# Residual sum kept in PSUM, and the norm placed right behind its root, at the entry of two feed-forward layers

## The chip, the cores and the metric

One core of a Trainium2 chip runs the whole program in a single launch. The metric is device time in microseconds (us), from which a median of three runs is taken. Five engines work side by side, each with its own in-order queue: TensorE (PE in the profile, with its weight loads as PEld), VectorE (DVE), ScalarE (ACT), GpSimd (POOL) and SyncE (SP), which here only starts transfers. Matmuls write to PSUM, the accumulator memory; the other data live in SBUF.

## The reference

Two transformer layers on one sequence of 1024 tokens with 1024 features, all in float32. The change sits where each layer goes from its token mixer to its feed-forward part:

```python
x = x + diff_attention(h, ...)        # layer 0;  layer 1: x + mla_attention(h, ...)
h = rms_norm(x, ffn_norm_g[i])
x = x + conv_ffn(h, w_up, conv_w, conv_b, w_down)

def rms_norm(x, g):
    xf = x.astype(float32)
    y = xf * rsqrt(mean(xf * xf, axis=-1, keepdims=True) + 1e-6)
    return y * g
```

The last step of each mixer is a product of its output with a 1024 by 1024 matrix `w_o`. So for each tile of 128 tokens the kernel needs the residual sum (x plus that product), its mean of squares, the normed tile, and the tile's transpose, which is the moving operand of the up-projection. The residual sum itself is needed again after the feed-forward part, and goes to HBM until then.

## The kernel before, in words

Every float32 product is made from three matmuls of a split operand: a high part (`self.hi`, a cast, line 127, on ACT as a rule) and a low part (`self.lo`, the difference, line 130, on DVE or POOL). Lines 119 to 121 (`mm3`) are the three matmuls. The up-projection is a Strassen-like scheme of seven products, so that operands which are sums and differences of blocks must be built too: `T1` to `T4` on the side of the tokens, `S1` to `S4` on the side of the weights.

The change is in `project_rest`, which runs once in each layer (about 510 to 570 us and 1680 to 1740 us of the span). Before it, half of the output product has been added to `X`. `project_rest` makes the other half, for the eight token tiles in the order 0, 4, 1, 5, 2, 6, 3, 7 (`tiles`). Iteration n of its loop handles three tiles at once:

- for tile n-2 (`older`), whose norm exists: PE transposes it (`turn`, line 812, eight 128x128 transposes into two PSUM banks), and the banks are split into operands. A tile of the first half of the tokens (`a_tile`) gives `B11` and `B21`: two casts on ACT (`high`) and two differences on DVE (`low`). A tile of the second half gives `B12` and `B22`: ACT copies B12 out (line 830), DVE forms `T1`, `T3`, `T2` and, for the first two of these tiles, `T4` (`sub`, line 843), and T1 is split at once, the low part on POOL; layer 1 does so with T2 as well.
- for tile n-1 (`before`): DVE adds the product in PSUM to the residual and writes the sum to SBUF (`add`, line 847), SP stores the sum to `x_d` (line 850), ACT sums its squares (`squares`, line 157), DVE takes the mean plus epsilon (line 164) and POOL the power -1/2 (`root`, line 167), and DVE multiplies sum, root and gain (line 916): the norm.
- for tile n: PE makes 24 matmuls into a two-bank PSUM tile (`ys[n] = self.big()`; there are two such tiles), behind the transposes of tile n-2.

Inside the loop the order on PE, DVE and POOL is the order of the program; the order on ACT and SP is planned by the scheduler from the dependencies. An instruction that waits holds up all that is behind it on its engine. On DVE the order in iteration n is: add, the first differences (low B11, or T1 and T3), line 164, the rest (low B21, or low B22, T2 and T4), one weight sum S in iterations 3 to 6 (line 1013), and then the norm. The sum lives in one of two SBUF places (`totals`); the norm goes to another place (`home`). The places of `totals` are used after the loop for split weights: the cast `w2h` of the closing order (a list of tokens, `CLOSE`, which begins behind the loop) writes where tile 6's sum was, and so it waits for that sum's store.

Tile 7 has no place in the loop any more: its sum, squares, root and norm are tokens of `CLOSE`, in halves.

Of the kernel before, what the change touches and what calls it, by code (L numbers as in the profile page):

```python
# [13 lines left out]
ALU = mybir.AluOpType  # L14
# [42 lines left out]
class Trunk:  # L57
# [28 lines left out]
    def at(self, place, shape, dt=F32):  # L86

        if isinstance(place, str):
            return self.t(self.mem, place, shape, 1, dt)
        size = int(np.prod(shape[1:]))  # L90
        piece = place[: shape[0], :size]
        if dt != F32:
            piece = piece.bitcast(dt)
        if len(shape) == 3:
            piece = piece.rearrange("p (a b) -> p a b", b=shape[2])
        return piece
# [684 lines left out]
    def project_rest(self, W, o_d, os, X, at, home, x_d, g, junk, places, sums, early, begin):  # L781
# [5 lines left out]
        nc = self.nc  # L787
        dve, gp = nc.vector, nc.gpsimd
# [3 lines left out]
        T, raws, ys, banks, tmp, r, ends = {}, {}, {}, {}, {}, {}, {}  # L792
# [3 lines left out]
        def load(n):  # L796
            if n < NT:
                raws[n] = self.project_load(tiles[n], ks, o_d, raw)

        def parts(n):  # L800
            return self.project_parts(raws.pop(n), ks, W, os)

        def normed(i, cols):
            return ends[cols.start] if i == NT - 1 else X[i][:, cols]

        def turn(i, which=3):
            names = ("B11", "B21") if i < 4 else ("B12", "B22")
            for name, cols in list(zip(names, (first, rest)))[which == 2 : which]:
                ps = banks[name, i % 4] = self.bank("u" if name == "B22" else "b")
                x = normed(i, cols)  # L810
                for k in range(4):
                    nc.tensor.transpose(ps[:, k * P : (k + 1) * P], x[:, k * P : (k + 1) * P], self.ident)

        def source(name, q):
            return cut(banks[name, q] if name[0] == "B" else tmp[name, q])

        def dst(name, q, part):
            if name not in T:
                T[name] = [self.at(place, [P, 4, 512], F32R) for place in places[name]]
            return T[name][part][:, :, q * P : (q + 1) * P]  # L820

        def high(name, q):
            self.hi(dst(name, q, 0), source(name, q))

        def low(name, q, eng=dve):
            self.lo(dst(name, q, 1), source(name, q), dst(name, q, 0), eng)

        def copy(q):
            tmp["B12", q] = sums([P, 512])
            nc.scalar.copy(tmp["B12", q], banks["B12", q])  # L830

        def sub(name, q):
            x, y = {
                "T1": lambda: (tmp["B12", q], banks["B11", q]),
                "T3": lambda: (banks["B22", q], tmp["B12", q]),
                "T2": lambda: (banks["B22", q], tmp["T1", q]),
                "T4": lambda: (banks["B21", q], tmp["T2", q]),
            }[name]()
            if name == "T1":
                tmp[name, q] = sums([P, 512])  # L840
            else:
                tmp[name, q] = normed(*{"T2": (q, first), "T3": (q + 4, first), "T4": (q + 4, rest)}[name])
            dve.tensor_sub(tmp[name, q], x, y)

        def add(i, y, cols=slice(0, D)):
            x, to = X[i]
            dve.tensor_add(to[:, cols], x[:, cols], y[:, cols])

        def store(i):
            nc.sync.dma_start(x_d[i * P : (i + 1) * P, :], X[i][1])  # L850

        def both(name, q, eng=dve):
            high(name, q)
            low(name, q, eng)
# [8 lines left out]
        for n, i in enumerate(tiles):  # L863
            into, ys[n] = ready, self.big()
            before = tiles[n - 1] if n else None
            older = tiles[n - 2] if n > 1 else None
            if older is not None:
                q, a_tile = older % 4, older < 4
                turn(older)
            into(ys[n][:, first], 0)  # L870
            into(ys[n][:, rest], 512)
            load(n + 2)
            if n + 1 < NT:
                ready = parts(n + 1)
            if before is None:
                continue
            X[before] = X[before], at(before, X[before])
            add(before, ys[n - 1])
            store(before)
            if older is not None:  # L880
                if a_tile:
                    high("B11", q)
                else:
                    copy(q)
                    if q or "B22" in early:
                        high("B22", q)
            s = self.squares(X[before][1], junk)
            if older is not None:
                if a_tile:
                    high("B21", q)  # L890
                    if older == 1 and "B22" not in early:
                        both("B22", 0)
                    low("B11", q)
                else:
                    sub("T1", q)
                    sub("T3", q)
            r[before] = self.root(s, D)
            if n in (4, 5):
                start.part(n - 4)
            if older is not None:  # L900
                if a_tile:
                    low("B21", q)
                else:
                    both("T1", q, gp)
                    if q or "B22" in early:
                        low("B22", q)
                    sub("T2", q)
                    if q < 2:
                        sub("T4", q)
                    if "T2" in early:  # L910
                        both("T2", q, gp)
            for name in {3: ("S1",), 4: ("S2",), 5: ("S4",), 6: ("S3",)}.get(n, ()):
                start.sum_of(0, name)
            x, total = X[before]
            X[before] = home(before, x)
            dve.scalar_tensor_tensor(X[before], total, r.pop(before), g, ALU.mult, ALU.mult)

        last, st = ys[NT - 1], SimpleNamespace()

# [1398 lines left out]
```

## Time and profile before

| | |
|---|---|
| median of 3 runs | 2379.11 us (2378.89 to 2379.76) |
| the profiled execution | 2379.93 us, of which the span from first to last instruction is 2378.1 us |
| granted TensorE clock | 0.999 of full speed |
| busy: PE, PEld, DVE, ACT, POOL | 2346.4, 1975.7, 1925.3, 1246.5, 587.5 us |
| line 916 (the norm), 14 times | min 1271, median 1572, max 2318 ns |

In a timeline row the columns are: start in us, duration in us, engine, line, operation, output<-inputs, count and, in brackets, how long the engine was idle before it and what released it. Names there are those of the places or banks: `u`, `s` and `h` are SBUF places, `S` is the two-bank PSUM tile, `b` is a PSUM bank. `u` is also the tag of one more PSUM bank (the one that takes B22), so that a `u` can be either. DVE instructions overlap a little: the next starts some 0.08 us before the end of the one before.

### The profile page before, as it was taken

The page shows a single profiled execution, that of the slowest core. Times are in us where ns is not written, and L with a number is a line of the kernel's source. Part 1 is how long each engine was busy: PE and PEld are TensorE (multiplying, and loading weights), DVE is VectorE, ACT ScalarE, POOL GpSimd, SP SyncE. Part 2 cuts the span into 40 slices and gives each one's busy share as a digit, 9 for nine tenths or more (in the row PEclk, how much of TensorE's full clock was granted, in tenths as well). Part 3 has the DMA queues.
Part 4 walks back from the last instruction along what each step waited for, and adds up shares of the span by engine and source line. Part 5 has one row for each costly group of instructions (what it writes and reads, how often), then busy time and mean ns, then how long its engine had stood idle before and what let it go on. Part 6 is the DMA issues. An engine that isn't in the chain of part 4 may idle for free.

```text
span 2378.1 us, 32958 instructions
## 1 busy us (share of the span) xinstructions
PE 2346.4 (99%) x12146; PEld 1975.7 (83%) x12146; DVE 1925.3 (81%) x3170; ACT 1246.5 (52%) x2301; POOL 587.5 (25%) x465
## 2 busy tenths in 40 slices
PE   9999999999999999999999999999999999999998
PEld 7888888788888888888898889988788888888886
DVE  6777877859888888999855888886588888889997
ACT  5666666745444444354444778775354444443544
POOL 4545444324000000000133666673420000000001
PEclk9999999999999999999999999999999999999999
DMA  3111111342222222652221211133322222227502
GB/s 148 40 36 36 49 37 54 114 130 86 93 84 80 80 88 81 233 176 84 84 98 56 72 33 39 41 98 114 108 72 94 82 80 80 89 80 283 177 1 80
DMA packets 95667, 213.42 MB, mean 90 GB/s; under 512 B 8713, under 2 KB 33937, under 8 KB 95505
## 3 DMA queue, kind: packets, MB, share of 16 engines
q1 hardware_dynamic: 86304, 183.51, 23.6%
q10 hardware_dynamic: 9200, 27.80, 3.2%
q8 instruction: 96, 1.57, 0.3%
q14 instruction: 67, 0.54, 0.1%
HBM read 158.85 MB, written 52.43 MB: 89 GB/s over the span
## 4 chain that ended last, share of the span: by engine, by line
PE 89%; DVE 5%; DMA 2%; ACT 2%; issue 1%; POOL 0%; POOLq 0%; DVEq 0%; ACTq 0%; SPq 0%
PE S L119 13%; PE S L121 13%; PE S L120 13%; PE b L119 9%; PE b L120 8%; PE b L121 8%; PE u L119 5%; PE u L121 4%; PE u L120 4%; PE S L1866 3%; PE b L263 2%; PE u L2022 1%; PE u L2021 1%; PE b L1912 1%; DVE s L130 1%
## 5 line engine op out<-in xcount | busy, mean ns | idle before, releaser
L167 POOL TENSOR_TENSOR st<-st,mhalf 128x1 f32<-128x1 f32 x56 | 35.4, 633 | 1301.5 <-DVE st L164 1291.4
L121 PE MATMUL S<-s,u 128*128 128x512 f32 (+1 forms) x800 | 301.3, 377 | 1.1 <-POOL u L130 1.0
L119 PE MATMUL S<-s,u 128*128 128x512 f32 (+1 forms) x800 | 301.8, 377 | 0.2 <-ACT u L1092 0.2
L120 PE MATMUL S<-s,u 128*128 128x512 f32 (+1 forms) x800 | 301.0, 376 | 0.0
L127 ACT CAST u<-h 128x512 fp32r<-128x512 f32 (+1 forms) x194 | 115.8, 619 | 274.4 <-DVE h L1013 262.2
L119 PE MATMUL b<-s,u 128*128 128x512 f32 x588 | 230.8, 393 | 1.1 <-DVE u L130 0.4
L120 PE MATMUL b<-s,u 128*128 128x512 f32 x588 | 229.0, 389 | 0.0
L121 PE MATMUL b<-s,u 128*128 128x512 f32 x588 | 229.0, 389 | 0.0
L1070 DVE SCALAR_TENSOR_TENSOR u<-u,conv,u 128x1023 f32<-128x1023 f32 (+1 forms) x176 | 225.0, 1278 | 0.8 <-ACT u L1066 0.7
L149 POOL TENSOR_TENSOR u<-u,st 128x512 f32<-128x512 f32 (+7 forms) x160 | 173.2, 1091 | 161.4 <-DVE st L2007 107.5
L127 ACT CAST s<-u 128x512 fp32r<-128x512 f32 (+3 forms) x229 | 144.0, 663 | 97.8 <-PE u L121 28.3
L127 ACT CAST u<-b 128x512 fp32r<-128x512 f32 (+1 forms) x256 | 134.8, 547 | 92.1 <-PE b L1912 57.7
L130 DVE TENSOR_TENSOR u<-b,u 128x512 fp32r<-128x512 f32 (+1 forms) x256 | 158.5, 631 | 23.7 <-ACT u L127 22.6
L121 PEld LDWEIGHTS S<-s,u 128*128 128x128 f32 x800 | 150.5, 188 | 29.2 <-POOL u L130 1.4
L119 PEld LDWEIGHTS S<-s,u 128*128 128x128 f32 x800 | 150.5, 188 | 27.9 <-ACT u L1092 0.5
L120 PEld LDWEIGHTS S<-s,u 128*128 128x128 f32 x800 | 150.6, 188 | 27.2
L119 PE MATMUL u<-s,s 128*128 128x512 f32 (+1 forms) x408 | 165.2, 405 | 1.1 <-DVE s L130 0.9
L121 PE MATMUL u<-s,s 128*128 128x512 f32 (+1 forms) x408 | 158.3, 388 | 0.0
L120 PE MATMUL u<-s,s 128*128 128x512 f32 (+1 forms) x408 | 157.6, 386 | 0.0
L130 DVE TENSOR_TENSOR s<-u,s 128x512 fp32r<-128x512 f32 (+2 forms) x205 | 140.7, 720 | 16.4 <-ACT s L127 15.9
L1073 ACT ACTIVATE u<-u 128x1024 f32<-128x1024 f32 x44 | 46.7, 1062 | 187.6 <-DVE u L1070 187.6
L130 DVE TENSOR_TENSOR u<-h,u 128x512 fp32r<-128x512 f32 x171 | 117.9, 689 | 32.4 <-ACT u L127 31.5
(290 smaller groups left out, 6384.9 us busy)
## 6 DMA issues: line engine op xcount, KB each, us to landing
u<-in_ffn_up SPq DMA_DIRECT2D x88, 512.0 KB, 4.2
g_d<-u ACTq DMA_DIRECT2D x44, 512.0 KB, 2.6
u<-in_ffn_down SPq DMA_DIRECT2D x66, 256.0 KB, 4.9
u<-g_d SPq DMA_DIRECT2D x62, 256.0 KB, 3.9
s<-in_da_wqkv SPq DMA_DIRECT2D x23, 512.0 KB, 3.3
x_d<-u SPq DMA_DIRECT2D x16, 512.0 KB, 3.0
s<-x_d SPq DMA_DIRECT2D x8, 1024.0 KB, 10.8
s<-g_d SPq DMA_DIRECT2D x18, 256.0 KB, 5.3
```

What stands on the lines that cost most here:

```text
L119: mm(out, lh, rl, start=first, stop=False, skip_group_check=onto)
L120: mm(out, lh, rh, start=False, stop=False, skip_group_check=onto)
L121: mm(out, ll, rh, start=False, stop=last, skip_group_check=onto)
L127: self.nc.scalar.copy(out, src)
L130: (eng or self.nc.vector).tensor_sub(out, src, hi.bitcast(F32))
L149: self.nc.gpsimd.tensor_mul(x, x, s.to_broadcast(list(x.shape)))
L167: nc.gpsimd.tensor_tensor(r, s, self.mhalf, ALU.pow)
L263: self.nc.tensor.transpose(ps[:, j * P : (j + 1) * P], probs[t][:, k : k + P], self.ident)
L1070: nc.vector.scalar_tensor_tensor(t[half][:, back:], u[half][:, : S - back], w, t[half][:, back:], ALU.mult, ALU.add)
L1073: nc.scalar.activation(t[0], t[0], AF.Silu)
L1866: nc.tensor.matmul(sc[c][:, b : b + m], q[rows, qp, qs], kt[rows, kp, :m], start=x == 0, stop=x == 2)
L1912: k.nc.tensor.transpose(ps[:, j * P : (j + 1) * P], self.e[t][0][:, c : c + P], k.ident)
```

## The change

The sum of tile n-1 is no longer written to SBUF by DVE. DVE adds the residual into the PSUM tile (`total`), ACT takes the squares from there and then copies the sum to its SBUF place, from which it is stored; the norm reads the PSUM tile too. The norm is moved up: for a second-half tile it now stands in front of T2, T4 and S, for a first-half tile in front of S. Tile 7, in the closing order, is as before.

```diff
-            X[before] = X[before], at(before, X[before])
-            add(before, ys[n - 1])
-            store(before)
+            total = ys[n - 1]
+            dve.tensor_add(total, X[before], total)
...
-            s = self.squares(X[before][1], junk)
+            s = self.squares(total, junk)
+            X[before] = X[before], at(before, X[before])
+            nc.scalar.copy(X[before][1], total)
+            store(before)
...
             r[before] = self.root(s, D)
             if n in (4, 5):
                 start.part(n - 4)
+
+            def norm():
+                X[before] = home(before, X[before][0])
+                dve.scalar_tensor_tensor(X[before], total, r.pop(before), g, ALU.mult, ALU.mult)
+
             if older is not None:
                 if a_tile:
                     low("B21", q)
                 else:
                     both("T1", q, gp)
                     if q or "B22" in early:
                         low("B22", q)
+                    norm()
                     sub("T2", q)
                     if q < 2:
                         sub("T4", q)
                     if "T2" in early:
                         both("T2", q, gp)
+            if older is None or older < 4:
+                norm()
             for name in {3: ("S1",), 4: ("S2",), 5: ("S4",), 6: ("S3",)}.get(n, ()):
                 start.sum_of(0, name)
-            x, total = X[before]
-            X[before] = home(before, x)
-            dve.scalar_tensor_tensor(X[before], total, r.pop(before), g, ALU.mult, ALU.mult)
```

## The prediction

> **What bounds the kernel now.** I read the page first, then PE's list of waits, then PE's timeline around the waits found there, and last the timelines of DVE, ACT and POOL beside it. On the page the busy line and the chain that ended last say which engine to follow:
>
> ```profile
> span 2378.1 us, 32958 instructions
> PE 2346.4 (99%) x12146; PEld 1975.7 (83%) x12146; DVE 1925.3 (81%) x3170; ACT 1246.5 (52%) x2301; POOL 587.5 (25%) x465
> PE 89%; DVE 5%; DMA 2%; ACT 2%; issue 1%; POOL 0%; POOLq 0%; DVEq 0%; ACTq 0%; SPq 0%
> ```
>
> PE is idle for about 2378.1 - 2346.4 = 32 us in all. An edit on other engines can win only such idle time. The longest total in the list of PE's waits is the one at issue:
>
> ```profile
> PE b L812 <- DVE u L916: 4.6, 4, 1.3
> ```
>
> The transposes (L812) waited four times for a norm (L916), 4.6 us. Idle time counts from the modelled end of a matmul, so I take what was lost from starts. First layer 0, then layer 1: the last matmul before a set of transposes, and the first transpose.
>
> ```profile
> 527.63 0.40 PE L121 MATMUL S<-s,h 128*128 128x512 f32 x1
> 527.87 0.60 PE L812 MATMUL b<-ident,u 128*128 128x128 f32 x4
> ...
> 534.00 0.39 PE L121 MATMUL S<-s,h 128*128 128x512 f32 x1
> 534.50 1.06 PE L812 MATMUL b<-ident,u 128*128 128x128 f32 x8
> ...
> 547.14 0.39 PE L121 MATMUL S<-s,h 128*128 128x512 f32 x1
> 548.87 1.06 PE L812 MATMUL b<-ident,u 128*128 128x128 f32 x8 [1.34 <-DVE u L916]
> ```
>
> ```profile
> 1702.15 0.39 PE L121 MATMUL S<-s,h 128*128 128x512 f32 x1
> 1703.86 1.06 PE L812 MATMUL b<-ident,u 128*128 128x128 f32 x8 [1.31 <-DVE u L916]
> ...
> 1716.51 0.39 PE L121 MATMUL S<-s,h 128*128 128x512 f32 x1
> 1718.22 1.06 PE L812 MATMUL b<-ident,u 128*128 128x128 f32 x8 [1.33 <-DVE u L916]
> ...
> 1730.71 0.39 PE L121 MATMUL S<-s,h 128*128 128x512 f32 x1
> 1731.69 1.06 PE L812 MATMUL b<-ident,u 128*128 128x128 f32 x8 [0.60 <-DVE u L916]
> ```
>
> Unhindered, the step is 527.87 - 527.63 = 0.24. The others are 0.50, 1.73, 1.71, 1.71 and 0.98, so 0.26 + 1.49 + 1.47 + 1.47 + 0.74 = 5.43 us are lost. All but the last come behind an iteration that ends with a weight sum; the large ones follow second-half tiles. The unhindered period of an iteration on PE is 534.24 - 527.87 = 6.37 us.
>
> Why the norm is late shows on DVE in iteration 5 of layer 0, with the ACT and POOL rows that it waits for or runs beside:
>
> ```profile
> 541.08 1.22 DVE L847 TENSOR_TENSOR u<-s,S 128x1024 f32<-128x1024 f32 x1 [0.17 <-PE S L121]
> 542.27 0.69 DVE L843 TENSOR_TENSOR h<-h,b 128x512 f32<-128x512 f32 x1
> ...
> 543.81 0.15 DVE L164 TENSOR_SCALAR st<-st 128x1 f32<-128x1 f32 x1 [0.25 <-ACT u L157]
> 543.88 0.68 DVE L130 TENSOR_TENSOR s<-u,s 128x512 fp32r<-128x512 f32 x1
> 544.48 0.68 DVE L843 TENSOR_TENSOR u<-u,h 128x512 f32<-128x512 f32 x1
> 545.20 0.69 DVE L843 TENSOR_TENSOR u<-b,u 128x512 f32<-128x512 f32 x1
> 545.80 0.68 DVE L1013 TENSOR_TENSOR h<-u,h 128x512 f32<-128x512 f32 x1
> 546.40 2.32 DVE L916 SCALAR_TENSOR_TENSOR u<-u,st,u 128x1024 f32<-128x1024 f32 x1
> 548.64 1.21 DVE L847 TENSOR_TENSOR u<-s,S 128x1024 f32<-128x1024 f32 x1
> ```
>
> ```profile
> 540.90 0.62 ACT L127 CAST h<-h 128x512 fp32r<-128x512 f32 x1 [3.61 <-issue]
> ...
> 542.62 1.07 ACT L157 ACTIVATE u<-u 128x1024 f32<-128x1024 f32 x1
> 543.58 0.20 ACT L157 ACTIVATION_READ_ACCUMULATOR u<-u 128x1 f32 x1
> ```
>
> ```profile
> 544.04 0.55 POOL L167 TENSOR_TENSOR st<-st,mhalf 128x1 f32<-128x1 f32 x1 [1.16 <-DVE st L164]
> ...
> 545.82 1.82 POOL L130 TENSOR_TENSOR s<-h,s 128x512 fp32r<-128x512 f32 x1
> ```
>
> The root is ready at 544.04 + 0.55 = 544.59, but the norm starts at 546.40, behind T2, T4 and S4, and then takes 2.32 us beside a POOL subtraction. From add to add this iteration costs DVE 548.64 - 541.08 = 7.56 us, more than PE's 6.37.
>
> **The change, part by part.** *The norm reads PSUM.* Whether that shortens it is told by DVE rows beside POOL, and by a row of the same operation with one operand in PSUM:
>
> ```profile
> 531.36 0.69 DVE L843 TENSOR_TENSOR u<-b,u 128x512 f32<-128x512 f32 x1
> 531.96 1.20 DVE L1013 TENSOR_TENSOR h<-u 128x512 f32<-128x512 f32 x1
> ```
>
> ```profile
> 531.32 1.30 POOL L130 TENSOR_TENSOR s<-h,s 128x512 fp32r<-128x512 f32 x1
> ```
>
> ```profile
> L439 DVE SCALAR_TENSOR_TENSOR u<-u,st,S x2: 1275/1278/1280, 7.2 to 8.4; 128x1024 f32<-128x1024 f32 x2
> ```
>
> Both DVE rows start under the POOL row. The one with a PSUM input keeps its 0.69, the one with two SBUF inputs takes 1.20 instead of 0.68. So I take 1.28 us for every norm, with 2.32 as the other end, and 1.20 for an S that lands beside POOL. The Trainium skill, page "SBUF — State Buffer", section "Who interferes with whom", says that a DVE instruction with two SBUF inputs contends with a GpSimd one that reads SBUF, and one with at most one SBUF input doesn't; these rows agree. By that rule the norm would be 1.28, without it 2.32 wherever POOL follows the root.
>
> *The norm is moved up.* It passes T2 and T4 (second-half tiles) and S. What it passes becomes later by the norm's 1.2 us: T4 frees the bank that the next first-half tile's B21 goes to, four transposes into its set, some 0.4 us behind the norm's own need.
>
> *The sum goes to PSUM in place.* Removed: the SBUF write of 14 adds. The add keeps its 1.22 us by row 541.08, which reads PSUM and writes SBUF. No row shows a DVE add that writes PSUM; the nearest is that row, and the other end is two passes, 2.44 us. I take 1.22. Squares from PSUM: at their 1.07 from SBUF; a 128x1024 activation out of `S` stands in this row at 1.118, so between 0 and +0.05 us each:
>
> ```profile
> L1891 ACT ACTIVATE u<-S,st 128x1024 f32<-128x1024 f32 x16 | 17.9, 1118 | 12.6 <-DVE st L1880 12.5
> ```
>
> *Added: 14 ACT copies of 128x1024*, at about 1.1 us by that row. ACT is half idle, so the copy matters only for who waits on it. First the norm: whether it may read the tile beside the copy no row shows; it starts at the end of the root at the earliest, at the end of the copy at the latest, 0.3 us apart (below). I take the later. Second the T1 cast behind it on ACT, whose product comes only behind the loop. Third the PSUM tile: it is free only when norm and copy are done, but the transposes in front of its next matmuls need the norm anyway: nothing. Fourth the store: it leaves some 2.4 us later (squares, copy). Behind it on SP stand loads of the next operands; the cast of one runs at 540.90 and its product only behind the transposes of 548.87, so 2.4 us are covered. The other user of the store is a rival below.
>
> *The walk.* Second-half iteration, from the add's start (rows of iteration 5): T1 and T3 end at 2.4; squares are read at 543.78 - 541.08 = 2.7; root ready at 3.5; copy 2.7 to 3.8; norm 3.9 to 5.2; T2, T4, S at 0.6 each: done at 6.9, against 7.56. First-half iteration, with two rows of iteration 6:
>
> ```profile
> 550.15 0.69 DVE L130 TENSOR_TENSOR s<-b,s 128x512 fp32r<-128x512 f32 x1 [0.30 <-ACT s L127]
> ...
> 551.69 0.15 DVE L164 TENSOR_SCALAR st<-st 128x1 f32<-128x1 f32 x1 [0.84 <-ACT u L157]
> ```
>
> The mean at 551.69 - 548.64 = 3.05, copy until 4.1, norm 4.2 to 5.4, S until 6.0. A pair takes DVE 6.9 + 6.0 = 12.9 us; PE takes 2 x 6.37 = 12.7. So the big stalls go, since norms end at 5.2 to 5.4 and are needed at about 6.2, but DVE runs up to half a microsecond behind PE. Late next are T4 in front of B21 (at 6.4 plus that lag, needed at 6.7) and the norm of iteration 6: I put 0.3 us per layer, 0.3 more in layer 1 where T2 is split on POOL and meets S, and 0.2 for the end of layer 1, where tile 7's chain starts earlier against PE by less than the 0.74 won: 1.1 us, at most 2.
>
> Sum: 5.43, and about 0.03 of slower restart behind each of five stalls (an estimate), 0.15, make 5.6 us on offer; less 1.1 that is 4.5 us. Both layers' following stages are PE's, so all of it reaches the end. The profiled execution took 2379.93, 0.82 above the median 2379.11; it would become 2375.4, the median 2374.6. A measurement of this kernel tells a difference of about 0.2%, 4.8 us, from none: the bound is 2374.35, just beside my value.
>
> **The rivals.** *All is won.* Copy and norm overlap, or the lag never reaches PE: 5.6 us, 2373.5. For it: without the wait for the copy a pair costs 12.9 - 2 x 0.3 = 12.3, under 12.7. Against it the Trainium skill, page "PSUM — Partial Sum Buffer", section "PSUM bank collisions raise a hardware error", has a rule: two engines may not touch one bank at once, two reads included. By it copy and norm must stand one behind the other, as I took for the sum; no run here shows it.
>
> *The later store holds up ACT.* The cast `w2h` waits for the store of tile 6's sum, and ACT's plan has it in front of the last copy of B12:
>
> ```profile
> 554.69 0.62 ACT L127 CAST u<-h 128x512 fp32r<-128x512 f32 x1 [3.04 <-DMA x_d<-u]
> 555.90 0.59 ACT L830 COPY h<-b 128x512 f32<-128x512 f32 x1 [0.59 <-PE b L812]
> ```
>
> ```profile
> DMA to landing us min/median/max: 2.6/3.0/5.9
> ```
>
> Now ACT is free 555.90 - 555.31 = 0.59 us before it is needed. With the store 2.4 us later and PE unhindered, the copy, the squares and the norm of tile 3 would come late by 0.6 to 3.5 us (landing 3.0 to 5.9) in each layer: 2 us twice, 2378.5. The planner orders ACT anew and will more likely put the cast behind the squares.
>
> *The wait is only handed on.* If ACT puts the 0.62 T1 cast in front of the copy, a pair costs 13.5, 0.8 over PE's; three pairs in two layers give 4.8 us back: 2379.
>
> *Slower.* The add in place reads and writes the same bank. With e us more per add a pair costs 12.9 + 2e, and six pairs lose 6 x (0.2 + 2e): the gain of 5.6 is gone at e = 0.37. With two passes (1.22) it is 6 x 2.6 = 15.8 - 5.6 = 10 us slower, 2389. Against it: plain adds into other places show no such cost.
>
> **How the numbers follow.** My case 0.45 (2373.8 to 2375.5), all won 0.20, the store 0.16, handed on 0.10, slower 0.09. Of my own case a bit over half lies below 2374.35, so faster 0.2 + 0.25 = 0.45; same 0.20 + 0.16 + 0.10 = 0.46; slower 0.09. The range of eight in ten runs from 2373.0, under which all stalls of the list are not enough, to 2379.2.
>
> **What would show it.** Right: no L812 waits for L916 over 0.3 us; norms all at 1.28; an ACT copy of 1.1 right behind each squares; adds still 1.22; S rows at 1.2 where POOL runs. Wrong: adds near 2.4; L812 waiting for L843 (T4) or for ACT's copy by over 1 us; an ACT row waiting for `x_d` ahead of the last L830 and a late norm of tile 3.

## The result, and the profile after

The changed kernel takes 2374.59 us, the median of 12 runs (2373.11 to 2376.89). The kernel before, run beside it, takes 2379.80 (2378.06 to 2381.29). The ratio is 0.9979 with a 95% interval of 0.9972 to 0.9987: about 5.2 us faster, just over the 0.2% that a measurement tells from no change. The profiled execution took 2374.86 us (before: 2379.93), at the same granted clock of 0.999. From its page, the span, the busy line and the chain that ended last:

```profile
span 2373.1 us, 32978 instructions
PE 2345.3 (99%) x12146; PEld 1975.3 (83%) x12146; DVE 1919.9 (81%) x3170; ACT 1259.3 (53%) x2315; POOL 584.3 (25%) x465
PE 91%; DVE 5%; DMA 1%; ACT 1%; issue 1%; POOL 0%; POOLq 0%; DVEq 0%; SPq 0%; ACTq 0%
```

The span is 5.0 us shorter and PE's busy time 1.1: most of what went, 3.9 us, is PE's idle time. In the list of PE's waits the entry of 4.6 us for the norm is gone (the norm is now line 905), and the transposes wait only at these places:

```profile
PE u L812 <- DVE h L945: 0.7, 2, 0.4
PE b L812 <- DVE u L843: 0.5, 1, 0.5
```

L945 is tile 7's norm in the closing order. PE's timeline, at the place that lost 1.49 us before, at the iteration behind it, and at the end of layer 1:

```profile
547.05 0.40 PE L121 MATMUL S<-s,h 128*128 128x512 f32 x1
547.28 1.04 PE L812 MATMUL b<-ident,u 128*128 128x128 f32 x8
...
553.42 0.39 PE L121 MATMUL S<-s,h 128*128 128x512 f32 x1
553.65 0.60 PE L812 MATMUL b<-ident,u 128*128 128x128 f32 x4
...
1725.97 1.03 PE L812 MATMUL b<-ident,u 128*128 128x128 f32 x8
...
1730.21 0.63 PE L812 MATMUL u<-ident,h 128*128 128x128 f32 x4 [0.33 <-DVE h L945]
```

The steps are 0.23 now, and 553.65 - 547.28 = 6.37 is the unhindered period. All fourteen such steps in the two loops read 0.23 or 0.24. DVE, ACT and POOL in the same iterations as those shown of before:

```profile
541.15 1.23 DVE L878 TENSOR_TENSOR S<-s,S 128x1024 f32<-128x1024 f32 x1 [0.81 <-PE S L121]
...
544.68 1.28 DVE L905 SCALAR_TENSOR_TENSOR u<-S,st,u 128x1024 f32<-128x1024 f32 x1 [0.22 <-ACT u L888]
...
547.21 0.68 DVE L1020 TENSOR_TENSOR h<-u,h 128x512 f32<-128x512 f32 x1
547.81 1.22 DVE L878 TENSOR_TENSOR S<-s,S 128x1024 f32<-128x1024 f32 x1
...
550.27 0.15 DVE L164 TENSOR_SCALAR st<-st 128x1 f32<-128x1 f32 x1 [0.65 <-ACT u L157]
...
551.25 1.28 DVE L905 SCALAR_TENSOR_TENSOR u<-S,st,u 128x1024 f32<-128x1024 f32 x1 [0.23 <-ACT u L888]
552.46 0.68 DVE L1020 TENSOR_TENSOR h<-u,u 128x512 f32<-128x512 f32 x1
553.85 1.23 DVE L878 TENSOR_TENSOR S<-s,S 128x1024 f32<-128x1024 f32 x1 [0.71 <-PE S L121]
```

```profile
543.55 1.03 ACT L888 COPY u<-S 128x1024 f32<-128x1024 f32 x1
...
554.28 0.59 ACT L830 COPY h<-b 128x512 f32<-128x512 f32 x1 [3.13 <-PE b L812]
554.77 0.63 ACT L127 CAST u<-h 128x512 fp32r<-128x512 f32 x1
```

```profile
544.46 1.29 POOL L130 TENSOR_TENSOR u<-u,u 128x512 fp32r<-128x512 f32 x1
```

The norm starts at 544.68, under a POOL subtraction that began at 544.46, and takes 1.28 us; before, it started 1.8 us later behind its add and took 2.32. DVE now waits for PE in front of the add (0.81, 0.71), where PE waited for DVE before.

The following table is worked out from the starts of transposes (L812) in the profiled executions. "Loop" runs from the first transposes of iteration 2 to those of tile 3 behind the loop, "tail" from there to the first ones of tile 7 in layer 1. The last two columns are the median of the runs and the ratio to the kernel before, run beside it on the same chip.

| kernel | loop, layer 0 | loop, layer 1 | tail | median us | ratio (95%) |
|---|---|---|---|---|---|
| before | 40.10 | 42.00 | 3.77 | 2379.80 | |
| changed | 38.07 | 38.09 | 4.24 | 2374.59 | 0.9979 (0.9972 to 0.9987) |
| move alone | 39.69 | 42.00 | 4.94 | 2380.70 | 1.0005 (0.9996 to 1.0014) |
| PSUM alone | 38.46 | 39.70 | 4.07 | 2376.43 | 0.9985 (0.9976 to 0.9994) |
| copy behind norm | 38.10 | 38.10 | 4.86 | 2374.80 | 0.9979 (0.9969 to 0.9988) |
| 1.8 us more on DVE per pair | 41.77 | 40.51 | 5.03 | 2381.61 | 1.0008 (0.9999 to 1.0017) |
| norm from the SBUF copy | 39.04 | 38.10 | 4.65 | 2376.03 | 0.9988 (0.9979 to 0.9997) |
| move, another place for w2h | 39.69 | 40.31 | 4.73 | 2378.74 | 0.9998 (0.9989 to 1.0007) |
| before, another place for w2h | 40.03 | 41.24 | 4.07 | 2379.32 | 1.0002 (0.9993 to 1.001) |

The loops give -2.03 and -3.91, the tail gives back 0.47. The rest of the 5.0 us is +0.39 ahead of the change, -0.17 between the two loops and +0.25 behind the tail; the start of the loop alone differs by more between executions (the last experiment). A loop in which nothing stalls takes 38.1 us, six periods of 6.35.

### The profile page after: what moved, and what is told of

Read it like the earlier page. It is cut to its first block, busy times and chain, and to the rows that moved or that the text cites. A ratio compares the mean times of both kernels' runs of the same rounds, so it can differ in the third digit from the quotient of the medians.

```text
span 2373.1 us, 32978 instructions
## 1 busy us (share of the span) xinstructions
PE 2345.3 (99%) x12146; PEld 1975.3 (83%) x12146; DVE 1919.9 (81%) x3170; ACT 1259.3 (53%) x2315; POOL 584.3 (25%) x465
## 4 chain that ended last, share of the span: by engine, by line
PE 91%; DVE 5%; DMA 1%; ACT 1%; issue 1%; POOL 0%; POOLq 0%; DVEq 0%; SPq 0%; ACTq 0%
PE S L121 14%; PE S L119 14%; PE S L120 14%; PE b L119 9%; PE b L120 8%; PE b L121 8%; PE u L119 5%; PE u L121 5%; PE u L120 4%; PE S L1873 3%; PE b L263 2%; PE u L2029 1%; PE u L2028 1%; PE b L1919 1%; DVE s L130 1%
## 5 line engine op out<-in xcount | busy, mean ns | idle before, releaser
L1077 DVE SCALAR_TENSOR_TENSOR u<-u,conv,u 128x1023 f32<-128x1023 f32 (+1 forms) x176 | 225.0, 1279 | 0.8 <-ACT u L1073 0.7
```

The lines of the kernel that those rows point to most:

```text
L1077: nc.vector.scalar_tensor_tensor(t[half][:, back:], u[half][:, : S - back], w, t[half][:, back:], ALU.mult, ALU.add)
```

## Experiments

The main theory: the norm was late for two reasons, the time it lost beside POOL and its place behind the differences and S; reading PSUM takes away the first, the move the second. The rivals: one of the two alone does it; ACT's new order does it (the cast `w2h` no longer waits for a store); or DVE merely has less to do.

**The move alone.** The norm stands behind its root as in the change, but reads the sum from SBUF, written there by DVE's add.

```diff
+            def norm():
+                x, total = X[before]
+                X[before] = home(before, x)
+                dve.scalar_tensor_tensor(X[before], total, r.pop(before), g, ALU.mult, ALU.mult)
...
+                    norm()
                     sub("T2", q)
...
+            if older is None or older < 4:
+                norm()
             for name in {3: ("S1",), 4: ("S2",), 5: ("S4",), 6: ("S3",)}.get(n, ()):
                 start.sum_of(0, name)
-            x, total = X[before]
-            X[before] = home(before, x)
-            dve.scalar_tensor_tensor(X[before], total, r.pop(before), g, ALU.mult, ALU.mult)
```

> The norm stands right behind its root as in the changed kernel, but the sum is written to SBUF by the add, as before, and squares, norm and store read it there. Theory 1 (both parts are needed: the order brings the norm forward, the PSUM operand keeps it at 1.28 us beside POOL): norms that run beside POOL take 2.3 us again, so T2, T4 and S slip; about 1.5 to 2 us of PE's 5.6 us of stalls come back, as waits of the transposes for T4 (L843) and for the norm: 3.5 to 4 us faster than before. Theory 2 (only the PSUM operand counts): no faster than before by more than 1 us. Theory 3 (only the order counts): as the changed kernel, 5 us faster.

It gains nothing: 2380.70 against 2379.41 beside it, where 3.5 to 4 us were expected. That alone is the value of the theory that only the PSUM operand counts; the next run speaks against it. Its group of norms, and one of them on DVE with what runs on POOL:

```profile
L904 DVE SCALAR_TENSOR_TENSOR u<-u,st,u 128x1024 f32<-128x1024 f32 x14 | 26.1, 1867 | 2.7 <-POOL st L167 2.0
...
544.75 2.30 DVE L904 SCALAR_TENSOR_TENSOR u<-u,st,u 128x1024 f32<-128x1024 f32 x1
...
548.30 1.72 DVE L1019 TENSOR_TENSOR h<-u,h 128x512 f32<-128x512 f32 x1
```

```profile
544.69 1.29 POOL L130 TENSOR_TENSOR u<-u,u 128x512 fp32r<-128x512 f32 x1
545.93 2.28 POOL L130 TENSOR_TENSOR s<-h,s 128x512 fp32r<-128x512 f32 x1
548.16 1.30 POOL L130 TENSOR_TENSOR h<-h,h 128x512 fp32r<-128x512 f32 x1
```

POOL makes the root, and its next subtraction starts 0.06 us ahead of the norm that waited for the same root. So the move puts the norm squarely under a POOL operation: 26.1 us for 14 norms, against 24.3 for line 916 before. POOL's next operation is stretched in turn and pushes its third under S4, which takes 1.72 instead of 0.68. The stalls are as large as before, at other iterations:

```profile
PE b L812 <- DVE u L904: 4.5, 5, 1.7
```

**PSUM alone.** The sum stays in PSUM, the norm stands where it stood.

```diff
-                    norm()
...
-            if older is None or older < 4:
-                norm()
             for name in {3: ("S1",), 4: ("S2",), 5: ("S4",), 6: ("S3",)}.get(n, ()):
                 start.sum_of(0, name)
+            norm()
```

> The sum stays in PSUM for squares, norm and copy, but the norm stands at its old place behind T2, T4 and S. Theory 1: norms take 1.28 us, so the three stalls of about 1.5 us shrink to about 0.5 and the others a little: 1.5 to 2 us of stalls stay, 3.5 us faster than before. Theory 2 (only the PSUM operand counts): as the changed kernel, 5 us faster. Theory 3 (only the order counts): within 1 us of before.

2376.43 against 2379.41: 3 us of the 5. It is 1.8 us behind the changed kernel, and 1.6 behind the next version, which ran beside it; its two loops are 2.0 us longer than those of the changed kernel. All norms take 1.27 to 1.28 us, also this one under POOL, but it is late for lack of the move, and PE still waits:

```profile
546.38 1.28 DVE L905 SCALAR_TENSOR_TENSOR u<-S,st,u 128x1024 f32<-128x1024 f32 x1
...
PE b L812 <- DVE u L905: 1.4, 3, 1.0
```

It starts 546.38 - 541.23 = 5.15 us behind its add, against 544.68 - 541.15 = 3.53 in the changed kernel. So PSUM carries the larger part, and the move is worth its 1.6 to 2.0 us only with it. The rival that DVE merely has less to do falls short too: the norms take as long in all here as in the changed kernel (17.9 and 18.0 us), and PE still waits.

**The copy behind the norm.** The norm runs straight behind the root; ACT's copy and the store follow it.

```diff
-            X[before] = X[before], at(before, X[before])
-            nc.scalar.copy(X[before][1], total)
-            store(before)
...
                 dve.scalar_tensor_tensor(X[before], total, r.pop(before), g, ALU.mult, ALU.mult)
+                nc.scalar.copy(place, total)
+                nc.sync.dma_start(x_d[before * P : (before + 1) * P, :], place)
```

> As the changed kernel, but the ACT copy of the sum and its store stand behind the norm in the program, so that the norm waits for the root alone and the copy for the norm. Theory 1 (norms had time to spare): norms start 0.2 to 0.3 us earlier, released by POOL, and the time stays within 0.7 us of the changed kernel; the store leaves 1.5 us later. Rival (the norm's wait for the copy still costs time): 1 to 3 us faster than the changed kernel. Rival (the later store holds up the cast that waits for it): ACT waits for x_d ahead of tile 3's squares, and 1 to 4 us of stall come back.

2374.80, ratio 0.9979 (0.9969 to 0.9988): the same as the changed kernel. Both loops are unhindered in both, so what the norm waits for the copy in the changed kernel (4.9 us in 14 times, 0.35 on average) costs nothing. Here the copy waits for the norm instead, 24 us in 14 times:

```profile
L904 ACT COPY u<-S 128x1024 f32<-128x1024 f32 x14 | 14.2, 1016 | 24.0 <-DVE u L903 24.0
...
1723.14 0.62 ACT L127 CAST u<-h 128x512 fp32r<-128x512 f32 x1 [1.59 <-DMA x_d<-u]
```

This version also shows the operand by itself. Eight of its norms start under a POOL subtraction, as many as in the move alone and as close behind its start, and all take 1.28 us, not 2.3. One of them, with POOL:

```profile
543.36 1.28 DVE L903 SCALAR_TENSOR_TENSOR u<-S,st,u 128x1024 f32<-128x1024 f32 x1
...
543.29 1.29 POOL L130 TENSOR_TENSOR u<-u,u 128x512 fp32r<-128x512 f32 x1
```

The end of layer 1 is 0.62 us later (the tail 4.86, not 4.24). ACT's plan has `w2h` and its wait for the store earlier, but that isn't the cause: tile 7's squares are done 2.33 us behind the start of tile 3's transposes in both kernels. What is longer is the difference `w2l`, which has two SBUF inputs, stands in front of tile 7's mean on DVE and runs beside a POOL subtraction. First this version, then the changed kernel:

```profile
1726.08 1.56 DVE L130 TENSOR_TENSOR u<-h,u 128x512 fp32r<-128x512 f32 x1
...
1727.38 0.94 DVE L130 TENSOR_TENSOR u<-h,u 128x512 fp32r<-128x512 f32 x1
```

**More work on DVE.** T1 is formed four times instead of once, which adds 3 x 0.6 = 1.8 us to DVE in each pair of iterations and nothing elsewhere.

```diff
+                    for _ in range(3):
+                        dve.tensor_sub(tmp["T1", q], tmp["B12", q], banks["B11", q])
```

> As the changed kernel, with the subtraction T1 made four times instead of once in each of the three second-half iterations of both layers: 1.8 us more on DVE per pair of iterations. In the trace of the changed kernel a pair takes DVE 11.9 us (6.66 from add to add, and 5.25 to the end of the sum in the next), PE 12.7. Theory 1 (DVE has 0.8 us per pair to spare and is the next bound): about 1.0 us lost per pair, less what the first pair hides: 3 to 6 us slower than the changed kernel, as waits for norm and T4. Rival (PE hides far more than that): within 1 us of the changed kernel.

2381.61, 7.0 us above the changed kernel: more than expected. From add to add a second-half iteration grew from 6.66 to 8.42 us, by 1.8 as meant. The loops grow by 3.70 and 2.42, and the tail and the end of layer 0 by 1.0. PE waits for the norm in eight places:

```profile
PE b L812 <- DVE u L907: 4.0, 8, 1.1
PE u L812 <- DVE h L947: 1.7, 2, 1.1
```

With about 0.8 us to spare per pair (below), 1.8 more leave 1.0 us over. That is what a pair shows once DVE is never idle in front of an add, here in layer 1:

```profile
1711.66 1.22 DVE L878 TENSOR_TENSOR S<-u,S 128x1024 f32<-128x1024 f32 x1
...
1720.08 1.22 DVE L878 TENSOR_TENSOR S<-u,S 128x1024 f32<-128x1024 f32 x1
...
1725.32 1.22 DVE L878 TENSOR_TENSOR S<-u,S 128x1024 f32<-128x1024 f32 x1
```

The pair takes 1725.32 - 1711.66 = 13.66 us, 0.96 over PE's 12.70. Three pairs of two layers would lose 6 us, and the loops lost 6.1, but that sum agrees partly by chance. Layer 1 lost only 2.42, since its first pair hides a part and its last isn't whole. Layer 0 lost 3.70, of which 1.27 are two weight sums that now land behind a POOL subtraction (0.88 and 1.75 us instead of 0.68):

```profile
536.45 0.88 DVE L1022 TENSOR_TENSOR h<-u 128x512 f32<-128x512 f32 x1
...
550.32 1.75 DVE L1022 TENSOR_TENSOR h<-u,h 128x512 f32<-128x512 f32 x1
```

DVE is the next bound here, close behind PE.

**The norm from the SBUF copy.** As the changed kernel, but the norm reads what ACT has copied.

```diff
-                dve.scalar_tensor_tensor(X[before], total, r.pop(before), g, ALU.mult, ALU.mult)
+                dve.scalar_tensor_tensor(X[before], copied, r.pop(before), g, ALU.mult, ALU.mult)
```

> As the changed kernel in everything (add in place, squares from PSUM, ACT copy, order), except that the norm reads the copy of the sum in SBUF. It waited for that copy already, so it starts at the same moment. Theory 1 (the operand in PSUM is what keeps the norm short beside POOL): norms take 2.3 us where POOL works behind the root, DVE falls behind by 1.0 us per norm, and 3 to 5 us of PE stalls come back: 2377.5 to 2379.5. Rival (what helps is the add and the squares in PSUM and the other plan of ACT): within 1 us of the changed kernel.

2376.03 is 1.4 us above the changed kernel, and so are loops and tail of the traces together; against the kernel before beside it (2378.90) it gains 2.9 us instead of 5.2. So 1.4 to 2.3 us are lost, between the two values of the expectation, which had 3 to 5 for the operand. The norms take 1535 ns on average, not the 1867 of the move alone. Two of them, and POOL beside them:

```profile
L906 DVE SCALAR_TENSOR_TENSOR u<-u,st,u 128x1024 f32<-128x1024 f32 x14 | 21.5, 1535 | 4.9 <-ACT u L888 4.9
...
532.46 1.28 DVE L906 SCALAR_TENSOR_TENSOR u<-u,st,u 128x1024 f32<-128x1024 f32 x1 [0.82 <-ACT u L888]
...
545.24 2.15 DVE L906 SCALAR_TENSOR_TENSOR u<-u,st,u 128x1024 f32<-128x1024 f32 x1 [0.23 <-ACT u L888]
```

```profile
532.95 1.95 POOL L130 TENSOR_TENSOR s<-h,s 128x512 fp32r<-128x512 f32 x1 [0.69 <-ACT s L127]
...
545.01 1.30 POOL L130 TENSOR_TENSOR u<-u,u 128x512 fp32r<-128x512 f32 x1
```

At 532.46 the norm starts first and keeps 1.28, and POOL's subtraction is stretched to 1.95. At 545.24 POOL is first, and the norm is stretched. ACT's copy stands ahead of the cast that POOL waits for, so that the norm is first more often than in the move alone. The expectation took over the contention of the move alone and left out that order. Only one loop stall remains, 0.75 us.

So the rival of ACT's new order holds a part of the truth: with the operand in SBUF, ACT's copy in front of the cast halves the norms that start second, from eight to four. With the operand in PSUM that order no longer matters, as the copy behind the norm shows.

**The place of w2h.** In layer 1 the places for split weights are dealt out in another order, so that `w2h` goes to a place that is free by then. Once with the move alone, once with the kernel before.

```diff
-            w=units(6, 7, 9, 8, 2, 3), sums=halves(9, 10, 11, 8, 3, 0), tmp=halves(1, 2, 4, 5, 6, 7), u=units(0, 1, 12, 13), t=units(10, 11),
+            w=units(6, 7, 2, 8, 9, 3), sums=halves(9, 10, 11, 8, 3, 0), tmp=halves(1, 2, 4, 5, 6, 7), u=units(0, 1, 12, 13), t=units(10, 11),
```

> The move alone once more (sum in SBUF), but in layer 1 the third split weight lies in another place (u2, free by then), so that its cast no longer waits for the store of tile 6's sum. In the move alone that wait (4.58 us of ACT) made tile 3's norm late, for stalls of 1.9 and 1.2 us at the end of layer 1. Theory 1 (the move alone fails by two things: norms of 2.3 us and this wait): 2.5 to 3 us faster than the move alone, so 1.5 to 2.5 us faster than before. Rival (the wait is only a symptom of a late DVE): within 1 us of the move alone.

> The kernel before, with that one other place in layer 1. ACT's wait of 4.7 us for the store goes, tile 3's norm starts about 1 us earlier, and PE's last stall of 0.74 us goes. Theory 1: 0.3 to 0.7 us faster than before, the rest of the stalls (4.7 us) unchanged. Rival (the wait for the store is a cause of the larger stalls too): 2 us faster or more.

With the move alone it gives 2378.74 against 2378.90 beside it: ratio 0.9998, where the move alone had 1.0005. The loop of layer 1 goes from 42.00 to 40.31, but four of the five stalls for the norm stay (3.0 us of 4.5), the norms take 1867 ns on average as in the move alone, and the tail keeps 0.96 of its 1.17 us over before. By the traces that is 1.9 us, by the ratios 1.7 with intervals that overlap, where 2.5 to 3 was expected. In the kernel before it takes the last stall of layer 1 away (the loop 42.00 to 41.24) and gives 0.3 back in the tail. The time, 2379.32 against 2378.90, can't be told from no change, where 0.3 to 0.7 us were expected:

```profile
PE b L812 <- DVE u L916: 4.0, 3, 1.3
```

The three large stalls are untouched, so the wait for the store is not what bound the kernel before, though it is a part of why the move alone gains nothing.

**The end of the layers.** In both kernels PE waits at tile 7's transposes in layer 0, in the changed one 0.42 and 0.55 us. A product of the up-projection, `p1b`, whose operands exist, is moved in front of those transposes; in a second version `p2a` is moved in the same way in layer 1 too (the last four lines).

```diff
-            "x w2h xa xs xb w2l xt xq B21.3h T2.1h T4.0h xr T2.0h B21.3l B11.3h eb ea T4.2s p1a p2a w3h yb",
-            "T2.1l w3g B11.3l ya B12.3c B22.3h T1.3s p1b T1.3h T3.3s T3.1h T3.0h p0a B22.3l T1.3l p0b T2.0g T2.3s p2b T4.3s T2.2h",
+            "x w2h xa xs xb w2l xt xq B21.3h T2.1h T4.0h xr T2.0h B21.3l B11.3h eb ea T4.2s p1a p2a p1b w3h yb",
+            "T2.1l w3g B11.3l ya B12.3c B22.3h T1.3s T1.3h T3.3s T3.1h T3.0h p0a B22.3l T1.3l p0b T2.0g T2.3s p2b T4.3s T2.2h",
...
-            "xa w2h T3.1h x p0a xb xs w2l xt xq xr B11.3h p1a eb yb B11.3l B21.3h ea p0b T4.0h w3h T4.2s B21.3l ya B22.3h",
-            "w3l c0 p2a T3.1l B22.3l w4h B12.3c T3.0h T1.3s T3.3s T3.0g T4.0g w4l p3a T2.3s T4.1h T1.3h T4.1l f1 w5h T2.3h",
+            "xa w2h T3.1h x p0a xb xs w2l xt xq xr B11.3h p1a p2a eb yb B11.3l B21.3h ea p0b T4.0h w3h T4.2s B21.3l ya B22.3h",
+            "w3l c0 T3.1l B22.3l w4h B12.3c T3.0h T1.3s T3.3s T3.0g T4.0g w4l p3a T2.3s T4.1h T1.3h T4.1l f1 w5h T2.3h",
```

> The changed kernel, with one token of the closing order of layer 0 moved: p1b (12 matmuls of 0.12 us, which need no part of tile 7) stands in front of the transposes of tile 7 instead of behind. They waited 0.42 us for tile 7's norm and 0.55 us for T4. Theory 1 (1.4 us of matmuls cover both waits): 0.5 to 1.0 us faster than the changed kernel. Rival (the transposes come 1 us later, and what follows them on DVE stalls PE instead): the same as the changed kernel or up to 1 us slower.

2373.53, ratio 0.9979 (0.9970 to 0.9988). Both waits are gone from its trace, and from tile 3's transposes in layer 0 to the first ones of layer 1's loop it takes 1126.45 us, where the other versions take 1127.3 to 1128.1:

```profile
563.80 0.60 PE L812 MATMUL u<-ident,h 128*128 128x128 f32 x4
564.24 0.60 PE L812 MATMUL b<-ident,h 128*128 128x128 f32 x4
```

To see whether that is a gain, it ran once more beside the changed kernel on one chip, with the second version:

> The changed kernel unaltered, on the same chip as the two versions beside it: 2374.6, 4.5 to 5.5 us faster than before.

> The version with p1b in front of the transposes of tile 7 in layer 0, next to the changed kernel. In its first trace both waits there (0.42 and 0.55 us) were gone and the way from the last loop transposes of layer 0 to layer 1 was 1.4 us shorter. Theory 1 (that is a real gain): 1.0 to 1.5 us faster than the changed kernel. Rival (the shorter way was chance): within 0.4 us of it.

> The same idea in layer 1 as well: p2a (1.4 us of matmuls without tile 7) in front of the transposes of tile 7, which waited 0.33 us for its norm, a wait that came with the change. Theory 1: that wait and the 0.24 us behind it go, 0.3 to 0.6 us faster than with layer 0 alone. Rival (p2a is missed as cover where it stood): 0 to 1 us slower than with layer 0 alone, with a new wait of PE at the start of the up-projection.

The changed kernel took 2374.07 (2373.31 to 2374.67), the end of layer 0 alone 2373.97 (2373.38 to 2374.57), both ends 2374.20 (2373.55 to 2376.38), with ratios of 0.9976, 0.9977 and 0.9979 and intervals of 0.001 to either side. The expected 1.0 to 1.5 us doesn't show in the times. In the traces the stretch between the loops is 1127.98, 1126.69 and 1126.92, so 1.1 to 1.3 us shorter there. Between profiled executions the start of layer 0's loop alone lies anywhere from 520.52 to 522.47, which is more. In the second version a wait of 1.5 us at the start of the up-projection takes the place of the one removed, which was the rival of its expectation:

```profile
PE u L119 <- DVE u L843: 1.5, 1, 1.5
```

Why the 1.2 us of the first version don't show in the median stays open. No version that beats the changed kernel was found.

## Why the prediction was right, point by point

The forecast was 2374.6, the median 2374.59. The mechanism came true, but that the hit is this close is luck. From profile to profile the forecast was 4.5 us, and it was 5.07 (2379.93 to 2374.86). Beside the changed kernel the one before had a median of 2379.80, 0.7 above the three runs that the forecast was based on, and that made up for a gain forecast too small. The chances don't follow from the sum either: a bit over half of the own case (2373.8 to 2375.5) was put below 2374.35, although the value, 2374.6, lies in its middle.

**On offer.** 5.43 us of late steps and 0.15 of slower restart were taken; the loops became 2.03 + 3.91 = 5.94 us shorter. Two steps of 0.31 that the sum left out hold 0.14 of the difference. The remaining 0.37, 0.07 a stall instead of 0.03, is put down to the restart by subtraction alone.

**The norm beside POOL.** 1.28 us for every norm was taken, with 2.32 as the other end. The group of after has 14 norms at 1284 ns on average, all that are under POOL included:

```profile
L905 DVE SCALAR_TENSOR_TENSOR u<-S,st,u 128x1024 f32<-128x1024 f32 x14 | 18.0, 1284 | 4.9 <-ACT u L888 4.9
```

That this is due to the operand in PSUM, and not to the place, is shown by the experiments: moved without PSUM 1867, PSUM without the move 1279, and 1535 where nothing but the operand differs from the changed kernel. The rule of the Trainium skill, page "SBUF — State Buffer", section "Who interferes with whom", holds in all of these. One sign did not come: a weight sum was to take 1.20 us where it lands beside POOL. All eight take 0.68, since in the changed kernel none of them starts second; POOL's subtraction is the longer one instead, twice (1.75 and 1.74 us, not 1.30).

**The copy.** 1.1 us was taken; it is 1.02 (14.2 us in 14, on average 1016 ns). The norm waits for it, as taken: that group's idle time, 4.9 us, is all for ACT's L888. That it costs nothing was not foreseen, and the experiment with the copy behind the norm shows it.

**The add in place.** 1.22 was taken, with 2.44 as the other end: 1.22 and 1.23. The slower rival needed 0.37 us more an add and falls. Squares from PSUM take 1.04 and 1.03, not more than the 1.07 from SBUF.

**The walk.** This is the step that was mis-sized. 6.9 us were forecast for a second-half iteration: 547.81 - 541.15 = 6.66. 6.0 were forecast for a first-half one: from the add at 547.81 to the end of S at 552.46 + 0.6 = 553.1, 5.25 us. The mean comes 550.27 - 547.81 = 2.46 behind the add, not 3.05. The row it was taken from, 551.69 of before, stood behind a stall of PE: there the transposes started at 548.87, behind the add at 548.64, and the casts and squares behind them; now they start at 547.28, ahead of the add at 547.81. So a pair takes DVE 11.9 us and not 12.9, under PE's 12.7: 0.8 to spare instead of 0.2 too much. The experiment with 1.8 us more bears the size out, by its pair of 13.66 us (11.9 and 1.8 make 13.7). So the 0.9 us put down for the loops (0.3 a layer, 0.3 for T2 on POOL) did not come.

**The tail.** 0.2 was put down for the end of layer 1; it gave back 0.47. Before, PE's stall in front of tile 3's transposes hid a part of tile 7's chain (add, squares, root, norm): tile 7's add began 0.22 us ahead of these transposes, at 1731.47; now it begins 0.20 behind them, at 1726.17. From that add to tile 7's norm it takes 3.14 us, 2.96 before, with `w2l` at 0.94 us beside POOL, 0.68 before. PE now waits 0.33 for the chain. In the move alone (tail 4.94) and the copy behind the norm (4.86) `w2l` takes 1.47 and 1.56, and from add to norm it takes 3.67 and 3.76.

**The rivals.** "All is won" gave 2373.5 on condition that copy and norm overlap or the lag never reaches PE: the second came true in the loops, while the tail took 0.47 of the 5.94 back; another 0.47 lies in the stretches outside, 0.39 of it ahead of the change. The later store didn't hold up ACT: the plan put `w2h` behind the last copy of B12 (554.28, then 554.77, with no wait for `x_d`). The prediction called a place behind the squares likely; it is still in front of those. The wait was not handed on: the copy at 543.55 comes straight behind the squares. Without the move, or without PSUM, the same sum would have failed: both are needed for the whole gain, which the prediction treated as one sum and didn't price apart.

## What to carry to other kernels

Where two engines share a resource, moving an instruction up to its releaser can place it exactly under the releasing engine's next operation; look at what that engine does next before counting the gain, and take away the shared operand together with the move. When a stalled loop is to be forecast without its stall, take the rows of the walk from an iteration behind no stall: a row taken behind one carries the stall's lateness with it. And keep account of the chain that ends the stage: a stall that is taken away in front of it no longer hides it.

## What the runs showed of the hardware

Not expected was that the contention has a winner: of a DVE operation with two SBUF inputs and a POOL subtraction, the one that starts first keeps its own time, and the other is longer by nearly the whole rest of the first. At 544.75 (move alone) the norm had 545.98 - 544.75 = 1.23 us of POOL's operation ahead of it and took 1.02 longer. At 545.93 POOL had 1.12 of the norm ahead of it and took 0.99 longer. At 548.30 S had 1.16 ahead and took 1.04 longer. At 532.95 (norm from the copy) POOL had 0.79 ahead and took 0.65 longer. The second pays the overlap less 0.12 to 0.21 us. The same holds for the other norms and weight sums with two SBUF inputs that overlap a POOL subtraction by more than 0.1 us in the loops of the kernel before, the move alone and the norm from the copy. The Trainium skill, page "SBUF — State Buffer", section "Who interferes with whom", states this rule (the issue order decides who blocks); the prediction used only its other half.

The copy and the norm, both readers of one PSUM tile, ran one behind the other in the changed kernel and in the version with the order reversed: the changed kernel's norm waits for the copy (4.9 us in 14 times, released by L888), and in the other the copy waits for the norm (24.0 us, released by L903). What two reads at once would do wasn't tried.
